# A trunk of two layers on one core: Toeplitz blocks loaded from a shifted copy in DRAM, or straight from the kernel table

## Chip, cores, metric

One core of a Trainium2 chip. The metric is device time in microseconds (us) of one execution, as the median of the runs; lower is better.

## What is computed

Two layers on 512 tokens of width 1024, each `x + Mixer(RMSNorm(x))`, and a final RMSNorm. The first mixer is chunked gated linear attention. The second is a state-space layer (S5) of 128 groups; a group has 16 channels and 64 complex states. The change concerns the second one alone:

```python
lam_bar = jnp.exp(lam * dt)
b_bar = ((lam_bar - 1.0) / lam)[..., None] * b_cplx
bu = einsum('blgi,gpi->blgp', u32, b_bar)              # 16 inputs of a group -> 64 states
_, states = associative_scan(combine, (a, bu), axis=1) # s_t = lam_bar * s_(t-1) + bu_t
y = real(einsum('blgp,gip->blgi', states, c)) + d_skip * u32
y = gelu(y); y = y * sigmoid(y @ w_glu + b_glu); y = y * silu(z)
out = y @ w_out
```

## The kernel before

**The S5 layer in pieces of eight tokens.** The 512 tokens are cut into 64 pieces of T = 8. The groups are worked in NB = 16 blocks of GB = 8 groups. For a group, `bm` (128 x 128) takes the 8 x 16 inputs of a piece to its states, a scan runs over the 64 pieces, `cm` (128 x 128) takes the state before a piece to its outputs, and `gh` (128 x 128) takes the inputs of a piece to the outputs of the same piece. `gh` is a Toeplitz matrix: its entry depends on output channel, input channel and the distance in time. All three are held as two fp16 parts (high and low), so a product is three matmuls (`three16`, lines 769 to 774).

**The kernel table.** `kz` in DRAM has for each group and input channel a row of 480 fp16 numbers: 224 zeros (distances below zero, written by `zero`, line 961) and then 256 values, the 8 distances x 16 outputs x (high, low). `finish_z` (line 1326) computes the 256 for one block: the four small products `pk` on TensorE at line 1333, evictions on ACT and VectorE, the split into `kf` on POOL (lines 1342 to 1345), and one 64 KB store at line 1346. The row of `gh` for input channel i at time j is row i of the table, read from 32 * j numbers further left: 256 numbers, 512 bytes.

**The shifted copy.** `gcopy` (line 1349) reads those 128 shifted rows for each of a block's 8 groups and writes them to `gmd`, an array in DRAM of 512 KB a block: one DMA, DRAM to DRAM. `load_b` (line 596) later loads a block of `gmd` through `loadw` (line 566) into SBUF, as one DMA of 512 KB (line 581), or for the first NPRE = 3 blocks as two of 256 KB (line 578), into the smaller `big` buffers. The same `loadw` loads `bm`, the scan tables `tab`, and `cm`.

**What sets the order.** The tables are prepared while the first layer runs: `plan` (lines 356 to 365) lists steps F (`finish_b`, `compute`, `load`), Z (`finish_z`, and `gcopy` of the block before), E (scan tables) and a last G (`gcopy` of block 15), and `hook` (line 369) takes steps at a rate (`RATES`) as TensorE's first-layer products are emitted. `compute` is POOL's work; its inputs `lpt`, `s_bi`, `s_xc`, `pp` come by DMA (lines 1276 to 1282). The second layer runs in steps too: `LAS`, `LBS` and so on give the step of each block's `load_a` (`bm`, `tab`), `load_b` (`gh`, `cm`), `sA` (first product, scan), `sB` (line 817: the products with `gh` and `cm`, then the store of y to `yd` on ACT's queue), `load_y` (line 834: y comes back from DRAM in another layout) and `sC` (line 839: GELU on ACT). Within a step, `rank` puts `load_y` ahead of `load_a` and `load_b`. Blocks 0 to 2 are loaded during the last of the first layer (lines 673, 674, 685 to 687). From this program order a compile-time scheduler, with an estimate of its own of how long each operation and transfer takes, fixes the order of instructions on each engine; an engine then works strictly in that order. Nearly all DMAs are issued by SP, also in order: one that waits holds all behind it. Weights go through `wunit` (line 178): two raw buffers (`wraw`), split into eight (`whl`) by ACT and VectorE or POOL.

Of the kernel before, what the change touches and what calls it, by code (L numbers as in the profile page):

```python
# [11 lines left out]
F16 = mybir.dt.float16  # L12
# [9 lines left out]
P = 128  # L22
# [9 lines left out]
T = 8  # L32
NC = SEQ // T
GB = 8
NB = 16
KW = 15 * 16
# [18 lines left out]
NPRE = 3  # L55
# [6 lines left out]
SEQ0 = 'h0 u h2 u h4 u s h6 u x0 t x1 q0 q1 t'  # L62
GP = 4
RATES = [0.84, 0.84, 0.88, 0.94, 0.94]
LOWS = {'F': 0, 'Z': 20, 'E': 100, 'G': 0}
ETABS = [2, 3, 3, 3, 3, 3, 3, 3, 4, 4, 4, 4, 4, 4, 4, 7, 8]
POS = [[0, 0, 1, 2, 1, 2, 3, 1, 2, 3, 3], [0, 1, 1, 3, 4, 5, 6, 5, 5, 7, 9], [0, 1, 3, 4, 4, 5, 6, 5, 6, 8, 8], [1,
    1, 4, 4, 4, 5, 6, 6, 6, 6, 8], [0, 0, 0, 0]]
# [22 lines left out]
def trunk_kernel(  # L91
# [6 lines left out]
    V, A, G, S, PE = nc.vector, nc.scalar, nc.gpsimd, nc.sync, nc.tensor  # L98
    sb = ctx.enter_context(tc.tile_pool(name="sb", bufs=1))
    ps = ctx.enter_context(tc.tile_pool(name="ps", bufs=1, space=PSUM))  # L100
    dr = ctx.enter_context(tc.tile_pool(name="dr", bufs=1, space=DRAM))
    cnt = [0]

    def T_(shape, tag, bufs, dt=F32):
        cnt[0] += 1
        return sb.tile(shape, dt, tag=tag, name=f"{tag}_{cnt[0]}", bufs=bufs)
# [20 lines left out]
    def q4(dt=F32, n=1024):  # L127
        return T_([P, n], "q4", Q4, dt)
# [204 lines left out]
    prep = S5Prep(tc, dr, C_, T_, PT, ident, q4, q2, big, tmp, s_bi, s_xc)  # L333
# [4 lines left out]
    @contextmanager  # L338
    def later(n):
        tc.cur_priority += n  # L340
        yield
        tc.cur_priority -= n
# [13 lines left out]
    plan = []  # L356
    ne = 0
    for cb in range(NB + 1):
# [3 lines left out]
        while ne < ETABS[cb]:  # L362
            plan.append(("E", ne))
            ne += 1
    plan.append(("G", NB - 1))
    pace = [0.0]
    phase = [0]

    def hook():
        pace[0] += RATES[phase[0]]  # L370
        while pace[0] >= 1:
            pace[0] -= 1
            if plan:
                st = plan.pop(0)
                with later(LOWS[st[0]]):
                    prep.step(mark, *st)
# [188 lines left out]

    def loadw(cb, src, dt=F16):
        n = 1024 if dt == F16 else 512
        if src is prep.gmd:
            srcs = [src[cb, 4 * k:4 * k + 4].rearrange("g p w -> p g w") for k in range(2)]
            full = src[cb].rearrange("g p w -> p g w")  # L570
        else:
            srcs = [src[cb][:, k * n:(k + 1) * n] for k in range(2)]
            full = src[cb]
        fit = (lambda t: t.rearrange("p (g w) -> p g w", w=2 * P)) if src is prep.gmd else (lambda t: t)
        if cb < NPRE:
            w = [T_([P, n], "big", BIG, dt) for _ in range(2)]
            for k in range(2):
                S.dma_start(out=fit(w[k]), in_=srcs[k])
            return w
        t = q4(dt, 2 * n)  # L580
        S.dma_start(out=fit(t), in_=full)
        return [t[:, :n], t[:, n:]]

    def wsel(w):
        return [[w[k][:, g * P:(g + 1) * P] for g in range(GB)] for k in range(2)]

    def gsel(w):
        v = [t.rearrange("p (g q k) -> p k g q", k=2, g=GB // 2) for t in w]
        return [[v[g // 4][:, k, g % 4] for g in range(GB)] for k in range(2)]

    def load_a(cb):
        t = st_[cb]
        t["bm"] = wsel(loadw(cb, prep.bmd))
        t["cs"] = loadw(cb, prep.tab, F32)

    def load_b(cb):
        t = st_[cb]
        t["gh"] = gsel(loadw(cb, prep.gmd))
        t["cm"] = wsel(loadw(cb, prep.cmd))

    v0 = ([], [])
# [35 lines left out]
    for h in range(NH):  # L637
# [26 lines left out]
        if h == 0:  # L664
            weave([z], tk)
            prep.zero()
            tick()
        elif h < NH - 1:
            weave([proj_v(h, *v), proj_out(h - 1, prev, range(2)), z], tk)
        else:  # L670
            weave([proj_v(h, *v), proj_out(h - 1, prev, range(1)), z], tk)
            weave([proj_out(h - 1, prev, (1,))], [(POS[4][b], trn, b) for b in range(4)])
            load_a(0)
            load_b(0)
# [7 lines left out]
    for n in range(2):  # L682
        phase[0] = 3
        weave([proj_out(NH - 1, prev, (n,))], [])
        for b in range(n + 1, NPRE if n else min(2, NPRE)):
            load_a(b)
            load_b(b)
        build_hT(xts, gc2, h23, l23, range(4 * n, 4 * n + 4), True, PT if n == 0 else PO)
        for tb in range(NT):
            square(xts[tb][n], ssq[:, tb, n:n + 1])  # L690
            S.dma_start(out=x1d[tb * P:(tb + 1) * P, n * 512:(n + 1) * 512], in_=xts[tb][n])
# [171 lines left out]
    def win():  # L863
        for c in ORDER:
            n = int(c[1])
            if c[0] == "u":
                yield from dense_tok(s_wu[n], h2, l2, lambda tb, acc, n=n: ev_u(n, tb, acc), late=False, pool=True)
            elif c[0] == "z":
                yield from dense_ch(s_wz[n], h2, l2, lambda m, acc, n=n: ev_z(4 * n + m, acc), pool=True)
            else:  # L870
                yield from dense_ch(w_glu[n], yh, yl, lambda m, acc, n=n: ev_g(4 * n + m, acc), pool=True)
# [6 lines left out]
    for b in range(NB):  # L878
        at(TS[b], sT, b)
        at(SRS[b], sR, b)  # L880
        at(A0S[b], sA, b)
        at(SBS[b], sB, b)
        at(SCS[b], sC, b)
        at(LYS[b], load_y, b)
        if b >= NPRE:
            at(LAS[b], load_a, b)
            at(LBS[b], load_b, b)
        at(SGS[b], s5, b)
    phase[0] = 4
    rank = {"sC": 0, "s5": 1, "sB": 2, "sA": 3, "sT": 4, "load_a": 5, "load_b": 6, "load_y": 4, "sR": 7}  # L890
    w = win()
# [22 lines left out]
    for tb in range(NT):  # L914
        for k in range(2):
            S.dma_start(out=f(x1p)[k * 64:(k + 1) * 64, 2 * tb:2 * tb + 2].rearrange("p q d -> p (q d)"),
                        in_=x1d.rearrange("(c j) d -> j c d", j=T)[2 * tb + k])
# [21 lines left out]
class S5Prep:  # L939
    def __init__(self, tc, dr, C_, T_, PT, ident, q4, q2, big, tmp, s_bi, s_xc):  # L940
        self.tc = tc
        self.nc = nc = tc.nc
        self.C_, self.T_, self.PT, self.ident = C_, T_, PT, ident
        self.q4, self.q2, self.big, self.tmp = q4, q2, big, tmp
        self.s_bi, self.s_xc = s_bi, s_xc
        self.kz = dr.tile([NG, 16, KW * 2], F16, name="kz")
        self.bmd = dr.tile([NB, P, 2 * GB * P], F16, name="bmd")
        self.cmd = dr.tile([NB, P, 2 * GB * P], F16, name="cmd")
        self.gmd = dr.tile([NB, GB, P, 2 * P], F16, name="gmd")
        self.tab = dr.tile([NB, P, 2 * GB * NC], F32, name="tab")  # L950
        self.pw = dr.tile([2 * NS, NG, 2 * T], F32, name="pw")
        self.lpt = dr.tile([T, NG, 2, NS], F32, name="lpt")
        self.bcd = dr.tile([2, NS, NG], F32, name="bcd")
        self.r8d = dr.tile([NS, NG], F32, name="r8d")
        self.kdd = dr.tile([NG, 16], F32, name="kdd")
        self.etd = dr.tile([NG], F32, name="etd")
        self.t = 0
        self.ld = {}
        self.res = {}
# [386 lines left out]
        S.dma_start(out=self.kz[cb * GB:(cb + 1) * GB, :, 224:480].rearrange("g i w -> (g i) w"),  # L1346
                    in_=kf.rearrange("p w k -> p (w k)"))

    def gcopy(self, cb):
        src = bass.AP(self.kz.tensor, self.kz[cb * GB].offset + 7 * 32, [[2 * KW, P], [-32, T], [1, 2 * P]])  # L1350
        self.nc.sync.dma_start(out=self.gmd[cb].rearrange("g (i j) w -> (g i) j w", j=T), in_=src)

    def step(self, mark, code, cb):
        with ExitStack() as st:
            for k in ("pe", "act", "dve", "sp"):
                st.enter_context(self.tc.issue_after(mark[k]))
            if code == "F":
                if cb:
                    self.finish_b(cb - 1)
                else:  # L1360
                    self.load(0)
                if cb < NB:
                    self.compute(cb)
                if cb + 1 < NB:
                    self.load(cb + 1)
            elif code == "Z":
                self.finish_z(cb - 1)
                if cb >= 2:
                    self.gcopy(cb - 2)
            elif code == "G":  # L1370
                self.gcopy(cb)
            else:
                self.etab(cb)

# [55 lines left out]
```

## Time and profile before

| | |
|---|---|
| median of 3 runs | 1055.71 us (1053.78 to 1055.98) |
| the profiled execution | 1054.56 us |
| its span, first to last instruction | 1052.9 us |
| mean granted TensorE clock | 0.945 |
| busy: TensorE, VectorE, POOL, ACT | 88%, 68%, 49%, 45% of the span |
| moved by DMA | 205.79 MB, mean 195 GB/s |

The engines are PE (TensorE matmul), PEld (its weight loads), DVE (VectorE), ACT (ScalarE), POOL (GpSimd) and SP (SyncE, which here only issues DMAs). A name such as SPq or ACTq means the engine's queue issuing a DMA. Tile names stand as output<-inputs, with buffer numbers left out, so `q<-gmd` is any load from `gmd` into a buffer of the kind `q4`. The first layer takes about the first 505 us; the blocks of the second run from about 545 to 815, and after that TensorE has the large products of `w_glu` and the output projection.

### The profile page before, as it was taken

To read this page: it belongs to the slowest core of one execution; us is meant where nothing else is said; L and a number is where in the kernel's file an instruction comes from. 1 tells how busy PE (TensorE), PEld (TensorE's weight loads), DVE (VectorE), ACT (ScalarE), POOL (GpSimd) and SP (SyncE) were. 2 spreads that over 40 slices of the span, in tenths; PEclk is the share of its full clock that TensorE was granted. 3 is DMA by queue.
4 is the path that set the end of the run, shared out by engine and by line. 5 is a ranking of instruction groups with operands and counts; after the bars stand their busy time and mean duration, and the time that the engine had idled before them with its cause. 6 is when DMAs were issued, how large, how long until landed. Compare 5 with 4: busy or idle time off the path is not lost. (4 is left out here: it accounts for less than half of the span.)

```text
span 1052.9 us, 13715 instructions
## 1 busy us (share of the span) xinstructions
PE 927.6 (88%) x5019; PEld 720.8 (68%) x5019; DVE 713.8 (68%) x916; ACT 472.2 (45%) x707; POOL 511.0 (49%) x477
## 2 busy tenths in 40 slices
PE   6795966699869796969989999999998999999996
PEld 5573754457646684747777777787777888888885
DVE  5794569957898887978645769789897432424322
ACT  5553343445546455433556684744453332313222
POOL 4164808976897979899973434453314000000000
PEclk9897987999889998989999999999999999999998
DMA  8884466999969899999578447687854323353312
GB/s 256 221 183 100 87 167 185 276 247 262 265 209 250 228 292 273 237 321 317 190 226 259 151 121 250 211 300 252 264 185 140 110 82 99 100 160 100 100 61 80
DMA packets 118707, 205.79 MB, mean 195 GB/s; under 512 B 32400, under 2 KB 69824, under 8 KB 118640
## 3 DMA queue, kind: packets, MB, share of 16 engines
q1 hardware_dynamic: 110208, 180.90, 55.2%
q0 software_dynamic: 5472, 19.02, 10.0%
q10 hardware_dynamic: 2960, 4.99, 1.3%
q8 instruction: 39, 0.64, 0.3%
q14 instruction: 28, 0.23, 0.1%
HBM read 167.69 MB, written 45.59 MB: 203 GB/s over the span
## 5 line engine op out<-in xcount | busy, mean ns | idle before, releaser
L162 DVE TENSOR_TENSOR whl<-wraw,whl 128x1024 fp32r<-128x1024 f32 x77 | 106.6, 1384 | 147.5 <-ACT whl L161 147.3
L161 ACT CAST whl<-wraw 128x1024 fp32r<-128x1024 f32 x100 | 104.7, 1048 | 183.7 <-PE pt L199 46.0
L202 PE MATMUL pd<-whl,actA 128*128 128x512 f32 x384 | 154.6, 408 | 12.9 <-ACT whl L161 9.2
L203 PE MATMUL pd<-whl,actA 128*128 128x512 f32 x384 | 154.2, 402 | 0.0
L204 PE MATMUL pd<-whl,actA 128*128 128x512 f32 x384 | 154.0, 404 | 0.0
L270 POOL TENSOR_TENSOR rstd<-rv,neghalf 128x1 f32<-128x1 f32 (+1 forms) x6 | 5.2, 874 | 248.4 <-DVE rv L269 248.4
L198 PE MATMUL pd<-actA,whl 128*128 128x512 f32 x256 | 101.6, 403 | 3.3 <-ACT u L732 3.1
L200 PE MATMUL pd<-actA,whl 128*128 128x512 f32 x256 | 101.4, 397 | 0.0
L202 PEld LDWEIGHTS pd<-whl,actA 128*128 128x128 f32 x384 | 74.4, 194 | 32.7 <-ACT whl L161 9.2
L202 PE MATMUL pd<-whl,q 128*128 128x512 f32 x192 | 80.3, 419 | 11.7 <-DVE xx L541 5.1
L204 PEld LDWEIGHTS pd<-whl,actA 128*128 128x128 f32 x384 | 73.9, 193 | 18.6 <-issue 2.8
L203 PEld LDWEIGHTS pd<-whl,actA 128*128 128x128 f32 x384 | 73.9, 192 | 17.7 <-issue 2.1
L162 POOL TENSOR_TENSOR whl<-wraw,whl 128x1024 fp32r<-128x1024 f32 x23 | 58.3, 2533 | 52.5 <-ACT whl L161 49.2
L203 PE MATMUL pd<-whl,q 128*128 128x512 f32 x192 | 79.6, 415 | 0.0
L1318 DVE TENSOR_TENSOR q<-q,q 128x1024 f16<-128x1024 f32 x32 | 60.4, 1886 | 12.6 <-ACT q L1317 12.3
L198 PEld LDWEIGHTS pd<-actA,whl 128*128 128x128 f32 x256 | 48.5, 190 | 16.6 <-ACT u L732 5.2
L1293 POOL TENSOR_TENSOR q<-q,q 128x1024 f32<-128x1024 f32 x16 | 43.4, 2709 | 31.7 <-DMA q<-s_bi 29.6
L198 PE MATMUL po<-actA,whl 128*128 128x512 f32 x128 | 52.4, 409 | 5.8 <-ACT whl L185 5.8
L185 ACT CAST whl<-wraw 128x1024 fp32r<-128x1024 f32 x36 | 37.7, 1046 | 44.0 <-PE pd L203 26.4
L200 PEld LDWEIGHTS pd<-actA,whl 128*128 128x128 f32 x256 | 48.4, 189 | 11.2
L204 PE MATMUL pd<-whl,q 128*128 128x512 f32 x128 | 53.7, 424 | 1.4 <-DVE q L165 1.4
L202 PEld LDWEIGHTS pd<-whl,q 128*128 128x128 f32 x192 | 38.4, 200 | 23.6 <-DVE xx L541 6.4
(334 smaller groups left out, 2484.4 us busy)
## 6 DMA issues: line engine op xcount, KB each, us to landing
wraw<-w_glu SPq DMA_DIRECT2D x32, 512.0 KB, 3.4
wraw<-w_v SPq DMA_DIRECT2D x16, 512.0 KB, 5.4
wraw<-w_z SPq DMA_DIRECT2D x16, 512.0 KB, 6.5
whl<-w_z POOLq DMA_DIRECT2D x16, 512.0 KB, 7.9
wraw<-w_out SPq DMA_DIRECT2D x16, 512.0 KB, 6.8
q<-lpt SPq DMA_DIRECT2D x16, 512.0 KB, 6.8
q<-s_bi SPq DMA_DIRECT2D x16, 512.0 KB, 9.5
tab<-q SPq DMA_DIRECT2D x32, 256.0 KB, 4.2
```

Of the source, the lines that this page charges most:

```text
L161: i0 = A.copy(out=dst_hi, in_=src)
L162: i1 = E.tensor_tensor(out=dst_lo, in0=src, in1=f(dst_hi), op=SUB)
L185: A.copy(out=hi, in_=raw)
L198: PE.matmul(acc, lhsT=wh, rhs=ah, start=first, stop=False)
L200: mark["pe"] = PE.matmul(acc, lhsT=wl, rhs=ah, start=False, stop=last).ins
L202: PE.matmul(acc, lhsT=ah, rhs=wh, start=first, stop=False)
L203: PE.matmul(acc, lhsT=ah, rhs=wl, start=False, stop=False)
L204: mark["pe"] = PE.matmul(acc, lhsT=al, rhs=wh, start=False, stop=last).ins
L270: G.tensor_tensor(out=dst, in0=v, in1=neghalf.to_broadcast([P, w]), op=ALU.pow)
L1293: tt(out=m, in0=lp, in1=bb, op=MUL)
L1318: nc.vector.tensor_tensor(out=hl[:, 1], in0=src, in1=hl[:, 0], op=SUB)
```

## The change

`gcopy`, the array `gmd` and the step G go. `load_b` gives `loadw` the table itself; for each of the block's eight groups one DMA of 64 KB reads the 128 shifted rows from `kz` into that group's 256 columns of the SBUF tile. The tiles, their buffers, the matmuls and all step tables stay. The program has 128 loads in place of 19, and 16 copies fewer.

```diff
--- before.py
+++ after.py
@@ -62,7 +62,7 @@
 SEQ0 = 'h0 u h2 u h4 u s h6 u x0 t x1 q0 q1 t'
 GP = 4
 RATES = [0.84, 0.84, 0.88, 0.94, 0.94]
-LOWS = {'F': 0, 'Z': 20, 'E': 100, 'G': 0}
+LOWS = {'F': 0, 'Z': 20, 'E': 100}
 ETABS = [2, 3, 3, 3, 3, 3, 3, 3, 4, 4, 4, 4, 4, 4, 4, 7, 8]
 POS = [[0, 0, 1, 2, 1, 2, 3, 1, 2, 3, 3], [0, 1, 1, 3, 4, 5, 6, 5, 5, 7, 9], [0, 1, 3, 4, 4, 5, 6, 5, 6, 8, 8], [1,
     1, 4, 4, 4, 5, 6, 6, 6, 6, 8], [0, 0, 0, 0]]
@@ -362,7 +362,6 @@
         while ne < ETABS[cb]:
             plan.append(("E", ne))
             ne += 1
-    plan.append(("G", NB - 1))
     pace = [0.0]
     phase = [0]
 
@@ -565,21 +564,20 @@
 
     def loadw(cb, src, dt=F16):
         n = 1024 if dt == F16 else 512
-        if src is prep.gmd:
-            srcs = [src[cb, 4 * k:4 * k + 4].rearrange("g p w -> p g w") for k in range(2)]
-            full = src[cb].rearrange("g p w -> p g w")
-        else:
-            srcs = [src[cb][:, k * n:(k + 1) * n] for k in range(2)]
-            full = src[cb]
-        fit = (lambda t: t.rearrange("p (g w) -> p g w", w=2 * P)) if src is prep.gmd else (lambda t: t)
         if cb < NPRE:
             w = [T_([P, n], "big", BIG, dt) for _ in range(2)]
+        else:
+            t = q4(dt, 2 * n)
+            w = [t[:, :n], t[:, n:]]
+        if src is prep.kz:
+            for g in range(GB):
+                S.dma_start(out=w[g // 4][:, g % 4 * 2 * P:(g % 4 + 1) * 2 * P], in_=prep.toep(cb * GB + g))
+        elif cb < NPRE:
             for k in range(2):
-                S.dma_start(out=fit(w[k]), in_=srcs[k])
-            return w
-        t = q4(dt, 2 * n)
-        S.dma_start(out=fit(t), in_=full)
-        return [t[:, :n], t[:, n:]]
+                S.dma_start(out=w[k], in_=src[cb][:, k * n:(k + 1) * n])
+        else:
+            S.dma_start(out=t, in_=src[cb])
+        return w
 
     def wsel(w):
         return [[w[k][:, g * P:(g + 1) * P] for g in range(GB)] for k in range(2)]
@@ -595,7 +593,7 @@
 
     def load_b(cb):
         t = st_[cb]
-        t["gh"] = gsel(loadw(cb, prep.gmd))
+        t["gh"] = gsel(loadw(cb, prep.kz))
         t["cm"] = wsel(loadw(cb, prep.cmd))
 
     v0 = ([], [])
@@ -946,7 +944,6 @@
         self.kz = dr.tile([NG, 16, KW * 2], F16, name="kz")
         self.bmd = dr.tile([NB, P, 2 * GB * P], F16, name="bmd")
         self.cmd = dr.tile([NB, P, 2 * GB * P], F16, name="cmd")
-        self.gmd = dr.tile([NB, GB, P, 2 * P], F16, name="gmd")
         self.tab = dr.tile([NB, P, 2 * GB * NC], F32, name="tab")
         self.pw = dr.tile([2 * NS, NG, 2 * T], F32, name="pw")
         self.lpt = dr.tile([T, NG, 2, NS], F32, name="lpt")
@@ -1346,9 +1343,8 @@
         S.dma_start(out=self.kz[cb * GB:(cb + 1) * GB, :, 224:480].rearrange("g i w -> (g i) w"),
                     in_=kf.rearrange("p w k -> p (w k)"))
 
-    def gcopy(self, cb):
-        src = bass.AP(self.kz.tensor, self.kz[cb * GB].offset + 7 * 32, [[2 * KW, P], [-32, T], [1, 2 * P]])
-        self.nc.sync.dma_start(out=self.gmd[cb].rearrange("g (i j) w -> (g i) j w", j=T), in_=src)
+    def toep(self, g):
+        return bass.AP(self.kz.tensor, self.kz[g].offset + 7 * 32, [[2 * KW, 16], [-32, T], [1, 2 * P]])
 
     def step(self, mark, code, cb):
         with ExitStack() as st:
@@ -1365,10 +1361,6 @@
                     self.load(cb + 1)
             elif code == "Z":
                 self.finish_z(cb - 1)
-                if cb >= 2:
-                    self.gcopy(cb - 2)
-            elif code == "G":
-                self.gcopy(cb)
             else:
                 self.etab(cb)
```

## Rows read from the trace of the kernel before

**Rows 1.** Windows by stage: start:end, length, busy us of each engine, granted clock, DMA share, GB/s.

```profile
200.00:458.00 258.00, 223.50 (x950) 164.58 (x949) 213.99 (x209) 127.50 (x195) 213.03 (x191) 0.92 0.91 253
458.00:560.00 102.00, 87.39 (x399) 67.99 (x398) 65.73 (x80) 50.97 (x86) 88.85 (x71) 0.92 0.82 257
560.00:800.00 240.00, 224.51 (x1952) 180.37 (x1951) 203.71 (x249) 129.27 (x181) 93.05 (x63) 0.99 0.67 219
800.00:1036.00 236.00, 236.00 (x1077) 190.11 (x1077) 83.45 (x91) 68.85 (x89) 6.74 (x4) 1.00 0.32 99
```

**Rows 2.** Waits of TensorE, 200 to 458 us: total us, times, longest.

```profile
PE pt L1333 <- POOL bh L1311: 7.6, 2, 5.4
PE pt L1333 <- DVE q L1323: 5.9, 1, 5.9
```

**Rows 3.** Waits of POOL, 200 to 458 us.

```profile
POOL q L1302 <- DMA pp<-pw: 13.3, 3, 6.2
...
POOL kf L1344 <- DMA kz<-kf: 6.7, 4, 3.1
```

**Rows 4.** DMA issues by line: KB each, median us from issue to landing.

```profile
gmd<-kz SPq DMA_DIRECT2D x16, 512.0 KB, 5.4
...
q<-gmd SPq DMA_DIRECT2D x13, 512.0 KB, 5.3
...
pp<-pw SPq DMA_DIRECT2D x16, 64.0 KB, 5.7
```

**Rows 5.** Tile gmd: issue durations in ns (least, median, most), first and last start.

```profile
L1351 SPq DMA_DIRECT2D gmd<-kz x16: 527/545/749, 218.9 to 555.9; - x16
L581 SPq DMA_DIRECT2D q<-gmd x13: 370/370/427, 569.1 to 776.7; - x13
L578 SPq DMA_DIRECT2D big<-gmd x6: 371/411/676, 460.8 to 492.7; - x6
```

**Rows 6.** Waits of the SP queue, whole span.

```profile
SPq L1351 <- DMA kz<-kf: 42.7, 11, 7.9
```

**Rows 7.** Timeline of SP, 316 to 332 us: start, us, queue, line, transfer.

```profile
321.21 0.33 SPq L1346 DMA_DIRECT2D kz<-kf  x1
328.60 0.54 SPq L1351 DMA_DIRECT2D gmd<-kz  x1
```

**Rows 8.** Timeline of SP, 125 to 155 us.

```profile
144.75 4.63 SPq L966 DMA_DIRECT2D kz<-tmp  x9
```

**Rows 9.** Timeline of TensorE, 775 to 777 us.

```profile
775.84 0.20 PE L772 MATMUL pt<-q,q 128*128 128x64 f16 x1
```

**Rows 10.** Timeline of SP, 744 to 757 us.

```profile
748.28 0.37 SPq L581 DMA_DIRECT2D q<-gmd  x1
...
750.00 0.47 SPq L836 DMA_DIRECT2D xx<-yd  x1
```

**Rows 11.** Timeline of SP, 457 to 487 us.

```profile
476.09 0.55 SPq L1278 DMA_DIRECT2D q<-s_bi  x1
...
477.31 0.54 SPq L1351 DMA_DIRECT2D gmd<-kz  x1
```

**Rows 12.** Timeline of POOL, 478 to 496 us, in brackets the idle time and its releaser.

```profile
485.67 2.40 POOL L1293 TENSOR_TENSOR q<-q,q 128x1024 f32<-128x1024 f32 x1 [0.41 <-DMA q<-s_bi]
```

**Rows 13.** Timeline of TensorE, 512 to 520 us.

```profile
517.09 0.89 PE L298 MATMUL pt<-ident,xx 128*128 128x128 f32 x4 [2.32 <-DVE actA L165]
```

**Rows 14.** Timeline of ACT, 757 to 800 us.

```profile
760.15 0.72 ACT L841 ACTIVATE big<-xx,mx 128x512 f32<-128x512 f32 x1 [2.57 <-DMA xx<-yd]
...
784.64 0.72 ACT L841 ACTIVATE big<-xx,mx 128x512 f32<-128x512 f32 x1 [4.45 <-DMA xx<-yd]
```

**Rows 15.** Timeline of TensorE, 786 to 796 us.

```profile
792.45 0.19 PE L773 MATMUL pt<-q,q 128*128 128x64 f16 x1 [3.56 <-DVE q L823]
```

**Rows 16.** Timeline of SP, 768 to 792 us.

```profile
776.75 0.37 SPq L581 DMA_DIRECT2D q<-gmd  x1
...
777.79 0.48 SPq L836 DMA_DIRECT2D xx<-yd  x1
```

## The prediction

> **What bounds the kernel now.** I read the windows first. [...] Then the waits of TensorE from 200 to 458: its first two rows, 7.6 and 5.9 us, are the small products of the table preparation, which wait for POOL and DVE [rows 2]; no row of that view names a DMA. The DMAs work at one remove: in the same stretch POOL waits 13.3 us for `pp` and 6.7 us for the landing of a `kz` store [rows 3]. Last the SP queue, which issues nearly every transfer in order.
>
> **What goes: sixteen copies inside DRAM.** Each moves 512 KB and takes 5.4 us to land [rows 4]; 11 of them are issued before 458, 5 from 458 to 556. Each issue holds SP for 0.545 us [rows 5], 8.7 us for all. Each also waits for the store of its own block, and while it waits SP issues nothing: 42.7 us in 11 waits [rows 6]. One such wait: store issued at 321.21, copy at 328.60 [rows 7]. For SP alone that is 51 us. I cost it at almost nothing: what covers it is that TensorE's waits of the stretch are all on engines [rows 2], and that weights are prefetched. What I do count is the traffic. 253 GB/s over 258 us is 65 MB, and the 11 copies are 5.8 MB of it, 9%, right behind the stores and loads that POOL waits for. Ends: 9% of POOL's 20.0 us, 1.8 us, if waits shrink only as bytes do; 13.5 us, TensorE's two waits for preparation, if POOL gets so far ahead that they vanish. I take 4, nearer the low end, because only the larger of the two is POOL's own, the other DVE's.
>
> **What comes: eight 64 KB loads for one of 512 KB (blocks 3 to 15), or for two of 256 KB (blocks 0 to 2).** Bytes and the 512-byte pieces stay the same. The new reads start every 64 bytes, as the copies' reads did; copies and loads of `gmd` land in 5.4 and 5.3 us [rows 4], so I cost the shifted reading at nothing. The added cost is issue time: nine small `kz` stores in a row took 4.63 us of SP, 0.51 each [rows 8], so eight cost 4.1 us, against 0.37 for one load or two times 0.41 [rows 5]. Per block that is 3.7 us more for blocks 3 to 15 and 3.3 for 0 to 2. Each load writes its own 256 columns; TensorE meets eight landings for one, at the first product of each group. No row prices seven waits that are already met; between nothing and 0.2 us a block (one such product takes 0.20 [rows 9]) I take nothing, since the loads come long before their use: the load at 748.28 [rows 10] is for block 13, whose product starts at 775.84 [rows 9], 27.6 us later.
>
> **458 to 560.** Blocks 0 and 1 are loaded here, before SP issues the inputs of the last preparation step: 12 more issues, 6.1 us, less one copy, 0.5, ahead of `s_bi` at 476.09 [rows 11]. POOL starts that step at 485.67, 0.41 us after it became free, the moment `s_bi` landed [rows 12]; its results go over DVE to the wait of 2.32 us before TensorE's transposes at 517.09 [rows 13]. There is no slack in that chain, so 5.6 us late at SP is 5.6 late on POOL. Against it stands the copy at 477.31 [rows 11], issued 1.2 us behind `s_bi` and sharing the engines with it: without it the landing is earlier, by nothing to its own 5.4 us. I take 1.6 and so 4 us later; ends 0 and, where small loads also hold each other up, 8.
>
> **560 to 800.** 13 times 3.7 is 48 us of SP's 240. Queued behind the eight are the `cmd` load, a weight load and the reload of `y`. The first two have cover: the use 26 us away and the split weights ahead of TensorE. The reload has none where ACT already stands waiting for it: before 760.15 for 2.57 us and before 784.64 for 4.45 us [rows 14], after which TensorE waits 3.56 us [rows 15]. Both reloads were issued just behind a Toeplitz load: 776.75 then 777.79 [rows 16], 748.28 then 750.00 [rows 10]. If all eight stay ahead, each comes 3.7 us later, 7.4 in all; if the scheduler, which has the reload as the older work, slips it in between, about nothing. I take one of the two, 3.7.
>
> **Sum**: -4 + 4 + 3.7 = **+3.7 us**. The profiled execution took 1054.56 us (span 1052.9 and 1.66 around it), 1.15 below the median of the three runs, 1055.71; the sum stands on the median: 1059.4, rounded to **1059 us**, slower by 0.3%. A measurement of this kernel tells about 0.2%, 2.1 us, from no change.
>
> **Rivals.**
> - Faster: the preparation was held up by traffic and by SP's 42.7 us, and both waits of 13.5 us go [rows 2]. For it: POOL is busy 83% of 200 to 458 and waits for transfers. Against it: other waits on the same engines (DVE behind ACT) stand next. With 13.5 won, the 4 of the second stretch and half a reload, 1.9: -7.6, so 1048. Chance 0.34, with the milder forms of it.
> - No change: the reloads are slipped in between, POOL's late step is paid by the missing copies, and 4 us are won and lost, or less. 1055.7; chance 0.20.
> - Slower by much more: both reloads late (7.4), the late step at its bound (8), nothing won: +15, 1071. It is the far end of my own case.
> - The change does not do only what it says: the order of all engines is built by a scheduler from its own estimate of transfers, so removing 16 and adding 109 issues can reorder work that the diff does not touch. Either sign; it widens each case by some 3 us and has no chance of its own.
> - The eight loads do not overlap. A 64 KB load like `pp` takes 5.7 us to land, no less than 512 KB in 5.3 [rows 4]; eight one after another are 45.6 us against the 27.6 between issue and use [rows 9, 10], so at least 18 us late, 1074 or more. Against it: the nine stores of [rows 8] were issued 0.51 us apart, far less than a landing. Chance 0.02. [...]
>
> **How the numbers follow.** Slower 0.46 (0.44 my own case, 0.02 loads that do not overlap), faster 0.34, same 0.20. My own case runs from 1058 to 1071. The range leaves out about one in ten on either side: 1047, just under the faster rival's 1048, to 1067, short of the far end.
>
> **What the next profile would show.** Right: no copies, 128 loads from `kz`, SP's waits for `kz` stores gone, eight issues in some 4 us; POOL's waits for `pp` and `kz` smaller; the `s_bi` wait near 485 longer by 4 us; ACT's waits for the `y` reload longer by 3.7 us at one place. I am wrong if TensorE's waits from 200 to 458 lose 8 us or more (the faster rival), if the reloads stand between the eight loads and no PE wait after 560 grows, or if TensorE waits for a Toeplitz load itself.

## The result, and the profile after

The changed kernel takes 1063.34 us (median of 20 runs, 1058.10 to 1074.18) against 1055.63 us for the kernel before (20 runs): a ratio of 1.0076, 95% interval 1.0053 to 1.0099, some 8 us slower. The ratio leaves out the execution of 1074.18, which ran in a slower state. The sign was forecast and the size, 1059, was low by 4 us; the way by which it came about was not the forecast one.

| | before | after |
|---|---|---|
| the profiled execution | 1054.56 us | 1059.76 us, 3.6 under its median |
| its span | 1052.9 us | 1058.1 us |
| mean granted TensorE clock | 0.945 | 0.941 |
| busy: TensorE, VectorE, POOL, ACT | 88, 68, 49, 45% | 88, 67, 47, 45% |
| moved by DMA | 205.79 MB | 197.42 MB |

The 8.4 MB that went are the sixteen copies (16 x 0.524 MB). The windows of the kernel after, by the stages of [rows 1]: length, busy us of PE, PEld, DVE, ACT and POOL, granted clock, DMA share, GB/s.

```profile
200.00:458.00 258.00, 216.41 (x894) 158.65 (x893) 206.35 (x204) 124.99 (x189) 210.24 (x188) 0.89 0.83 227
458.00:560.00 102.00, 87.69 (x401) 67.35 (x400) 65.53 (x85) 45.33 (x82) 77.54 (x68) 0.92 0.76 241
560.00:800.00 240.00, 228.11 (x1970) 183.66 (x1970) 195.84 (x243) 133.39 (x186) 87.56 (x64) 0.99 0.67 212
800.00:1036.00 236.00, 234.20 (x1088) 189.88 (x1085) 89.30 (x95) 71.78 (x94) 13.32 (x8) 1.00 0.33 105
```

The loss is in the first row. The DMA share fell from 0.91 to 0.83, and yet TensorE got through 894 instructions instead of 950, busy 216 us instead of 223, at a clock of 0.89 instead of 0.92. From 560 on it is, if anything, quicker than before. TensorE ends its 1400th instruction at 434.8 us instead of 423.3, so by then 11.5 us are lost. A landmark farther on says nearly the same: the eight one-column products that turn the row scales (line 698 before, 696 after) stand between the two layers. Their line in the view of one source line, with the first and the last start, before:

```profile
L698 PE MATMUL pt<-ident,big x8: 245/245/266, 543.1 to 543.9; 1*128 1x1 f32 x8
```

and after:

```profile
L696 PE MATMUL pt<-ident,big x8: 245/245/266, 551.7 to 552.5; 1*128 1x1 f32 x8
```

The first layer ends 8.6 us later; the rest of the span is 506.4 us (1058.1 - 551.7) instead of 509.8. So the two terms that I had put into the time after 458 are not what was lost: from the 1400th instruction on, the changed kernel is the quicker one. The waits of TensorE from 200 to 458 after, to be held against [rows 2]:

```profile
PE pt L1330 <- POOL bh L1308: 8.8, 1, 8.8
PE pt L407 <- DVE q L165: 7.2, 1, 7.2
PE po L202 <- ACT big L164: 5.3, 2, 4.1
PE pd L203 <- DMA whl<-w_v: 4.2, 1, 4.2
```

and those of POOL, against [rows 3]:

```profile
POOL whl L187 <- ACT q L164: 9.1, 1, 9.1
POOL bh L1306 <- PE pt L1330: 8.6, 2, 6.5
POOL tmp L1340 <- DVE tmp L1336: 6.5, 2, 5.1
...
POOL kf L1341 <- DMA kz<-kf: 2.6, 2, 2.2
...
POOL q L1299 <- DMA pp<-pw: 2.2, 2, 2.1
```

POOL's waits for transfers did what I had hoped: `pp` from 13.3 to 2.2, `kz` from 6.7 to 2.6. But POOL now stands behind ACT, TensorE and VectorE instead, and TensorE waits longer for POOL than before. All of TensorE's waits in this stretch add up to 41.6 us, before to 36.2; those of the small products alone fell, from 13.8 to 8.8, so what grew are its waits for weights and for the engines that split and evict.

Where that wait comes from can be read in POOL's timeline. The small product of a preparation step needs the factor `bh` of its block, which has one buffer. After:

```profile
283.46 3.24 POOL L1290 TENSOR_TENSOR q<-q,q 128x1024 f32<-128x1024 f32 x1 [4.02 <-DVE q L1320]
...
294.18 0.45 POOL L1306 TENSOR_TENSOR bh<-big,BA 128x128 f32<-128x128 f32 x1
...
295.99 1.43 POOL L1308 TENSOR_TENSOR bh<-bh,bh 128x128 f32<-128x128 f32 x1
```

and before:

```profile
284.39 1.39 POOL L1309 TENSOR_TENSOR bh<-big,BA 128x128 f32<-128x128 f32 x1
285.85 1.36 POOL L1311 TENSOR_TENSOR bh<-bh,bh 128x128 f32<-128x128 f32 x1
```

The same `bh` is ready at 287.2 before and at 297.4 after, though POOL waits less for transfers: in the compiled order of the kernel after, the first products of a later step now stand ahead of it, and the first of them waits 4.02 us for VectorE. TensorE, after:

```profile
297.48 1.06 PE L1330 MATMUL pt<-q,bh 128*32 128x256 f32 x2 [8.77 <-POOL bh L1308]
...
311.63 0.63 PE L202 MATMUL pd<-whl,q 128*128 128x512 f32 x1
312.06 0.57 PE L203 MATMUL pd<-whl,q 128*128 128x512 f32 x1
312.46 0.40 PE L204 MATMUL pd<-whl,q 128*128 128x512 f32 x1
312.70 0.40 PE L202 MATMUL pd<-whl,q 128*128 128x512 f32 x1
```

More is lost here than the 8.77 us of the wait. Behind it the 512-column products start 0.43 us apart, up to 312.1; from 312.5 they start 0.24 apart. The granted clock of the two stretches was 0.50 and 1.00:

```profile
297.40:312.40 15.00, 9.59 (x26) 5.57 (x27) 10.37 (x15) 3.11 (x7) 15.00 (x18) 0.50 0.54 167
312.40:330.00 17.60, 17.60 (x78) 11.62 (x77) 15.58 (x16) 10.23 (x15) 15.33 (x14) 1.00 0.42 120
```

The kernel before has a wait of this kind too, of 5.45 us before 300.80, and a granted clock of 0.51 in the 5.0 us behind it.

Of the order: the diff leaves the program order of TensorE, VectorE, ACT and POOL as it was. But the compile-time scheduler builds each engine's order from its own estimate of the transfers. The two traces first differ on SP at 218.9 us, where the kernel before issues its first copy, and on the other engines between 228 and 231. The longest sequence that both traces share has 387 of POOL's 477 instructions, 831 of VectorE's 916 and 4758 of TensorE's 5019.

### The profile page after: what moved, and what is told of

The parts are those of the page before. It is cut to its first block, busy times and chain, and to the rows that moved or that the text cites. A ratio compares the mean times of both kernels' runs of the same rounds, so it can differ in the third digit from the quotient of the medians.

```text
span 1058.1 us, 13800 instructions
## 1 busy us (share of the span) xinstructions
PE 929.9 (88%) x5019; PEld 723.5 (68%) x5019; DVE 704.9 (67%) x916; ACT 471.5 (45%) x707; POOL 499.4 (47%) x477
## 2 busy tenths in 40 slices
DMA packets 103812, 197.42 MB, mean 187 GB/s; under 512 B 33888, under 2 KB 54928, under 8 KB 103744
## 5 line engine op out<-in xcount | busy, mean ns | idle before, releaser
L162 DVE TENSOR_TENSOR whl<-wraw,whl 128x1024 fp32r<-128x1024 f32 x77 | 110.2, 1431 | 157.2 <-ACT whl L161 157.0
L161 ACT CAST whl<-wraw 128x1024 fp32r<-128x1024 f32 x100 | 104.8, 1048 | 203.3 <-PE pd L203 43.5
L202 PE MATMUL pd<-whl,actA 128*128 128x512 f32 x384 | 155.7, 410 | 13.8 <-ACT whl L161 9.2
L202 PE MATMUL pd<-whl,q 128*128 128x512 f32 x192 | 81.6, 426 | 18.7 <-DVE big L165 9.1
L1315 DVE TENSOR_TENSOR q<-q,q 128x1024 f16<-128x1024 f32 x32 | 70.8, 2212 | 23.5 <-ACT q L1314 22.4
L203 PE MATMUL pd<-whl,q 128*128 128x512 f32 x192 | 80.4, 420 | 0.0
L204 PE MATMUL pd<-whl,q 128*128 128x512 f32 x128 | 54.6, 433 | 0.1
```

What stands on the lines that cost most here:

```text
L161: i0 = A.copy(out=dst_hi, in_=src)
L162: i1 = E.tensor_tensor(out=dst_lo, in0=src, in1=f(dst_hi), op=SUB)
L202: PE.matmul(acc, lhsT=ah, rhs=wh, start=first, stop=False)
L203: PE.matmul(acc, lhsT=ah, rhs=wl, start=False, stop=False)
L204: mark["pe"] = PE.matmul(acc, lhsT=al, rhs=wh, start=False, stop=last).ins
L1315: nc.vector.tensor_tensor(out=hl[:, 1], in0=src, in1=hl[:, 0], op=SUB)
```

## The experiments

Three explanations were to be told apart: the eight issues crowd SP (mine); taking the copies out does harm by itself, for instance because SP's waits no longer hold other transfers back; the new compile-time order does the harm.

**e1, the loads alone.** The changed kernel with the copies put back, their target read by nobody (the array, the calls and the step G come back too and are not printed).

```diff
+    def gcopy(self, cb):
+        src = bass.AP(self.kz.tensor, self.kz[cb * GB].offset + 7 * 32, [[2 * KW, P], [-32, T], [1, 2 * P]])
+        self.nc.sync.dma_start(out=self.gmd[cb].rearrange("g (i j) w -> (g i) j w", j=T), in_=src)
```

> The copies stay (their target is no longer read); the Toeplitz blocks come from the table by eight transfers each. The compile-time order of TensorE's work is that of the kernel before for its first 1493 instructions, past 500 us. If the eight issues crowd SP's queue (ahead of the last preparation input and of the y reloads), this run carries the loss: about 1063, +8 us. If the loss comes from taking the copies out (the first layer in another order), this run is within 2 us of the kernel before, 1054 to 1058, with first-layer windows (200 to 458: PE 223, clock 0.92) as before.

Measured: 1053.73 us, ratio 0.998 (0.9949 to 1.0011). The eight issues, as the scheduler places them, cost nothing that can be told from no change.

**e2, the copies gone alone.** One transfer a block (two for blocks 0 to 2), from `cmd`, so that the product is made of other values.

```diff
-            for g in range(GB):
-                S.dma_start(out=w[g // 4][:, g % 4 * 2 * P:(g % 4 + 1) * 2 * P], in_=prep.toep(cb * GB + g))
+            def piece(g0, ng):
+                return bass.AP(prep.cmd.tensor, prep.cmd[cb].offset + g0 * P * 2 * P,
+                               [[2 * P, P], [P * 2 * P, ng], [1, 2 * P]])
...
+                S.dma_start(out=fit(t), in_=piece(0, GB))
```

> The copies go; the Toeplitz blocks are fetched by one transfer (two for blocks 0 to 2) in the same 512-byte pieces from another array written by then, so the Toeplitz product is made of other values. TensorE's order is that of the changed kernel for its first 1541 instructions. If the eight issues are the cost, this run is no slower than before, 1052 to 1056 (my -4). If taking the copies out is the cost, it is slow by about as much as the changed kernel, 1060 to 1064, and the first TensorE product of the second layer's input (line 696) starts near 551 us instead of 543.

Measured: 1062.68 us, ratio 1.0059 (1.0025 to 1.0094), with the same 8.77 us wait for `bh`, here at 298.55. Taking the copies out carries the loss, by itself or by the order that comes with it.

**e3 and e4, one priority changed.** The constant `'Z': 20` becomes 10 in the kernel before and 30 in the changed one.

> The kernel before, with one constant of the order changed (the z half of a preparation step is put 10 instead of 20 behind in the scheduler's priorities): same work, same transfers, another compile-time order. If order by itself is worth several us here, it moves by 3 us or more in either direction (1047 to 1063); if it is worth little, it stays within 2 us of 1055.6.

> The changed kernel with the same constant at 30 instead of 20: same work and transfers, another order. If the 8 us are a matter of the order that the scheduler happened on, some of it comes back or more is lost, 3 us or more away from 1063.3; if they belong to the removal of the copies or to the eight issues themselves, it stays at 1061 to 1066.

Measured: e3 1052.11 us, 0.997 (0.9938 to 1.0001); e4 1066.88 us, 1.0107 (1.0065 to 1.0149). e3 is level with the kernel before, near the faster edge; e4 lost nothing certain and won nothing back.

**e5 and e6, the copies made short.** As e1, with copies of 8 KB in e5 (printed here against e1), and in e6 of 1024 pieces of 4 bytes instead of 512.

```diff
-        src = bass.AP(self.kz.tensor, self.kz[cb * GB].offset + 7 * 32, [[2 * KW, P], [-32, T], [1, 2 * P]])
-        self.nc.sync.dma_start(out=self.gmd[cb].rearrange("g (i j) w -> (g i) j w", j=T), in_=src)
+        src = bass.AP(self.kz.tensor, self.kz[cb * GB].offset + 7 * 32, [[2 * KW, 16], [1, 2 * P]])
+        self.nc.sync.dma_start(out=self.gmd[cb, 0, 0:16], in_=src)
```

> As e1 (eight loads, copies kept), but each copy moves 8 KB instead of 512 KB, from the same array and with the same wait for the block's store; the order of TensorE's products of preparation is like that of the changed kernel (third and fourth step's products 31 matmuls apart or less, the third at matmul 842 instead of 809). If the loss comes from SP no longer being held back by the copies' waits, this run has the waits and is fast: 1052 to 1056. If it comes from the compile-time order, it is slow, 1060 to 1066, with TensorE's wait for bh of some 8 us near 297.

> As e5, but each copy has all its 1024 pieces, of 4 bytes instead of 512 (4 KB a block): bytes of the copies gone, waits kept, and an order in which the third preparation step's products stand at matmul 809 as in the kernel before, the fourth's at 843 and 855. Order theory: no 8 us wait near 297, and 1050 to 1056, the bytes saved counting for at most a few us. If the copies' bytes had mattered to POOL as my faster rival has it, 1045 to 1050. If this run is slow (1060 or more), order is not the cause.

Measured: e5 1078.79 us, 1.018 (1.0118 to 1.0242); e6 1062.35 us, 1.0081 (1.0047 to 1.0116). In both SP still issues sixteen copies and waits for stores ahead of them (27.5 us in e5, 38.1 in e6), so what held SP back is there, and both are slow: the loss does not need the waits to be missing. e5 lies beyond the 1060 to 1066 that I expected, with executions from 1066.65 to 1083.95; why it is so much slower than the changed kernel was not tried. And e6 speaks against the order theory in the narrow form that I gave it: the third step's products stand where they stood before, and the time was not won back.

**e7 and e8, the changed kernel with the bh chain loosened.** In e7 `'Z'` is 50; in e8 `bh` has two buffers.

```diff
-        bh = self.C2([P, GB, 16], "bh")
+        bh = self.T_([P, GB, 16], "bh", 2, F32)
```

> The changed kernel with the z half of a preparation step put 50 instead of 20 behind: no copies, no waits, but the third and fourth step's products at matmuls 811 and 845 and the fifth's at 919, spread as in the kernel before. Order theory: the 8 us wait near 297 goes and the time is that of the kernel before within some 3 us, 1051 to 1058. If SP's missing waits or the missing copies are the cause, it stays at 1061 to 1066.

> The changed kernel with two buffers instead of one for the small left factor bh of the table's product: POOL can make the next step's bh before TensorE's products of the step before. If the loss is the chain product, bh, product through one buffer, the wait of 8.8 us near 297 goes and with it 5 us or more: 1053 to 1059. If bh only stands late in POOL's queue for other reasons, the wait stays and so does the time, 1061 to 1066.

Measured: e7 1063.36 us, 1.0072 (1.0041 to 1.0103); e8 1060.24 us, 1.0042 (1.0013 to 1.0072). The wait of 8.77 us shrank to 5.43 in e7, with others of the kind behind it, and went in e8, where TensorE's timeline has another in its place:

```profile
295.44 0.80 PE L492 MATMUL pt<-big,big 128*128 128x128 f32 x2 [5.35 <-DVE big L162]
```

So the narrow theory, one wait for one buffer, falls: e7 won nothing and e8 no more than half. What was still open was whether the whole order costs it, or the absence of the copies.

**e9 to e11, the same work in another's order.** The order of a build can be held: an order-only edge (no semaphore) from each instruction of an engine to the next, along a list read from another build. So the changed work ran in the order of the kernel before (e9) and in that of e3 (e11), and the work before in the order of the changed kernel (e10).

```diff
+def in_order(tc):
+    ...
+    for e, order in table.items():
+        for k, n in zip(order, order[1:]):
+            tc.add_manual_dep(lists[e][n], lists[e][k].name, no_sync, reason="order")
```

> The changed kernel's work (no copies, eight loads a block), with every engine's instructions held by order-only edges in the order of the kernel before; on SP the copies are left out and the eight loads stand together where the one load stood. If the compile-time order is the cause, it is as fast as the kernel before or a little faster, 1049 to 1057, and the windows from 200 to 458 show PE's clock at 0.92 or more. If the missing copies or their missing waits are the cause themselves, it stays at 1061 to 1066.

> The work of the kernel before (sixteen copies, one load a block), with every engine held in the order of the changed kernel; each copy stands right behind the store of its block on SP, each single load where the first of the eight stood. If the order is the cause, it is as slow as the changed kernel or slower, 1060 to 1070, with TensorE's 8.8 us wait for bh near 297. If the copies' presence is what keeps the kernel before fast, it is at 1052 to 1057.

> As e9, but in the order of e3 (the kernel before with one priority changed), which ran 0.3% under the kernel before. If the order carries over to the changed work, 1047 to 1055, and this is the fastest of all; if the missing copies cost by themselves, 1058 to 1064.

Measured: e9 1067.61 us, 1.0116 (1.0075 to 1.0157); e10 1070.22 us, 1.0154 (1.011 to 1.0199); e11 1061.36 us, 1.007 (1.0039 to 1.0101). By the totals e10 bears the order theory out, and e9 and e11 contradict it. The traces show why: they lose at another place. The first layer of e9 is back, its landmark at 545.6:

```profile
L696 PE MATMUL pt<-ident,big x8: 245/245/266, 545.6 to 546.4; 1*128 1x1 f32 x8
```

while the rest of its span is 520.9 us (1066.5 - 545.6) against 509.8. There the eight loads had been held together, and SP's timeline and ACT's show the reload of y behind them:

```profile
788.56 5.67 SPq L574 DMA_DIRECT2D q<-kz  x8
...
794.90 0.43 SPq L834 DMA_DIRECT2D xx<-yd  x1
```

```profile
769.37 0.72 ACT L839 ACTIVATE big<-xx,mx 128x512 f32<-128x512 f32 x1 [3.83 <-DMA xx<-yd]
799.42 0.72 ACT L839 ACTIVATE big<-xx,mx 128x512 f32<-128x512 f32 x1 [9.98 <-DMA xx<-yd]
```

These are the two places of [rows 14], 2.57 and 4.45 us there. From 545 to 830 us (e9 has one more behind it, 4.4 us before 834), ACT's waits for reloads add up to 23.3 us in e9; before, 15.4; in the changed kernel, whose scheduler put reloads between the loads, 9.7. The rows are from ACT's waits in e9, before and after:

```profile
ACT big L839 <- DMA xx<-yd: 23.3, 6, 10.0
```

```profile
ACT big L841 <- DMA xx<-yd: 15.4, 5, 4.5
```

```profile
ACT big L839 <- DMA xx<-yd: 9.7, 5, 3.0
```

**e12, both at once.** e1 has nearly the order of the kernel before in the first layer, and the scheduler's own mixing of loads and reloads in the second. The changed work was held in e1's order, the copies alone left out.

> The changed kernel's work with every engine held in the order of e1 (which kept the copies, ran level with the kernel before, and has the y reloads standing between the eight loads); on SP only the copies are left out. In e9 the first layer came back (TensorE's instruction 1900 ended at 547 us, 553 in the changed kernel) and the second layer lost, with ACT waiting 27.7 us for y reloads queued behind eight loads instead of 15.4. If those two are all there is, this run is level with the kernel before or faster by what the copies' traffic was worth, 1048 to 1056, y-reload waits near e1's 9.5 us. If taking the copies away costs something by itself, it is at 1059 or more.

Measured: 1047.65 us, ratio 0.9946 (0.9923 to 0.9968). It is faster than both kernels, by some 6 us and some 14. The row of its landmark, and SP's timeline with a reload between the loads:

```profile
L696 PE MATMUL pt<-ident,big x8: 245/245/266, 537.0 to 537.8; 1*128 1x1 f32 x8
```

```profile
744.31 4.01 SPq L574 DMA_DIRECT2D q<-kz  x5
...
749.04 0.38 SPq L834 DMA_DIRECT2D xx<-yd  x1
...
750.56 1.80 SPq L574 DMA_DIRECT2D q<-kz  x3
```

**All of them side by side.** The windows view for 270 to 430 us shows what an order is worth: same 160 us, TensorE's busy time and instruction count first, then PEld, DVE, ACT, POOL, the clock, DMA share, GB/s. Before, e9 and e12:

```profile
270.00:430.00 160.00, 135.95 (x591) 100.83 (x590) 136.78 (x138) 77.30 (x121) 141.16 (x125) 0.91 0.89 252
```

```profile
270.00:430.00 160.00, 136.10 (x584) 101.80 (x584) 142.91 (x140) 77.15 (x121) 140.27 (x125) 0.89 0.82 228
```

```profile
270.00:430.00 160.00, 134.39 (x590) 99.53 (x589) 142.22 (x141) 78.95 (x122) 143.04 (x127) 0.91 0.81 227
```

After, e8 and e10:

```profile
270.00:430.00 160.00, 130.09 (x535) 95.25 (x535) 127.51 (x128) 75.75 (x117) 136.43 (x122) 0.87 0.81 223
```

```profile
270.00:430.00 160.00, 127.90 (x542) 95.23 (x543) 130.49 (x133) 75.31 (x119) 133.47 (x116) 0.87 0.79 217
```

```profile
270.00:430.00 160.00, 126.14 (x517) 92.19 (x517) 114.87 (x118) 72.86 (x113) 129.32 (x112) 0.87 0.85 239
```

584 to 591 instructions in the old order, with copies or without; 517 to 542 in the new ones, with copies (e10) or without. The orders themselves fall apart in the same way: of POOL's 477 instructions, 425 to 477 share the sequence of the kernel before in e1, e3, e9, e11 and e12, and 374 to 391 in the changed kernel, e2, e4 to e8 and e10. e6, which has the third step in its old place, is among the latter with 391, so it was no test of the old order. The same for a fixed amount of work: each trace holds 5019 records of TensorE, and the table takes the time between the ends of two of them by their number, with the idle time in it. Neighbours differ a little between orders, but 550 and 2100 instructions are nearly the same work. Each row is one execution: that of e11 (1067.15) was 5.8 us above its median and that of e7 (1058.21) 5.2 below.

```
                       850th to 1400th     2100th to 4200th    ratio of
                       us     idle us      us     idle us      the runs
before                 150.4  24.1         271.9  14.3
e3                     149.5  25.5         273.6  14.5         0.997
e1                     150.7  22.7         271.2  13.5         0.998
e12                    145.4  21.2         269.5  12.1         0.9946
e9  (loads together)   146.7  20.5         282.3  18.1         1.0116
e11 (loads together)   154.5  29.8         283.0  18.9         1.007
after                  164.5  29.9         268.9  13.0         1.0076
e2                     165.8  32.1         273.1  14.2         1.0059
e4                     165.8  29.6         269.4  11.1         1.0107
e5                     165.4  36.0         271.8  12.3         1.018
e7                     163.5  30.0         266.8  10.9         1.0072
e8                     161.5  31.5         269.3  13.1         1.0042
e10 (copies kept)      172.6  35.9         266.5   9.5         1.0154
```

The first pair of columns knows two kinds of kernel, 145 to 155 us in orders that a scheduler made with the whole copies in sight, 161 to 173 in orders made without them or with short ones; whether the copies then run or not (e9, e11, e12 without them, e10 with them) does not change the kind. Part of the 14 us between before and after is idle time (5.8); in the rest nearly the same products took longer, at a granted clock of 0.87 instead of 0.91 in the windows above. The stretches that the table leaves out are not alike either: up to the 850th the kernel before takes 262.9 us, the changed one 260.3 and e12 256.2, and from the 1400th to the 2100th 158.3, 156.3 and 165.4. So some of a gain or loss in the first columns is given back behind them, and at the landmark the changed kernel is 8.6 us behind the kernel before and 14.7 behind e12. The second pair knows two kinds as well: 267 to 274 us, and 282 to 283 where the eight loads are held ahead of the reloads.

## Why the prediction was right in sign, and where it was wrong

**That 1059 came so near is luck.** None of its three terms is what made the changed kernel slower, and what did was put at no chance.

**Copies, -4: not contradicted, and not shown.** e12 and e1 have the same order and the same loads and differ in the copies. The quotient of their ratios, 0.9946 / 0.998 = 0.9966, is -3.6 us, and by their two intervals it may be anything from -7.6 to +0.4. The traces of other pairs in one order do not agree. At TensorE's 1400th instruction e9 is 4.0 us ahead of the kernel before (419.3 and 423.3), but e11 is 4.9 behind e3 (425.2 and 420.3). Nor did the gain come as I had it, by way of POOL: its waits for transfers from 200 to 458 us add up to 21.9 us in e9 and 21.7 before, and TensorE's waits for the small products to 14.1 and 13.8. No run takes SP's 42.7 us of waits for stores [rows 6] out by themselves; what they cost is in the -3.6. The faster rival's time, 1048, is that of e12, but not by its mechanism: in e12 TensorE still waits 6.7 and 6.6 us for the preparation, where [rows 2] have 7.6 and 5.9.

**What comes, the issues.** I took 0.51 us an issue from small stores [rows 8]. The view of the tile `kz` after gives 0.60 (least, median, most in ns):

```profile
L574 SPq DMA_DIRECT2D q<-kz x104: 514/597/1826, 578.8 to 792.0; - x104
L574 SPq DMA_DIRECT2D big<-kz x24: 514/597/729, 473.9 to 506.4; - x24
```

So a block's eight cost 4.8 us of SP, not 4.1. TensorE never waited noticeably for a Toeplitz load (0.3 us in all in that view), and the rival in which the loads do not overlap is out: e12's second stretch in the table, 269.5 us, is no longer than the 271.9 before. And e1, which exchanges one transfer for eight, has a ratio of 0.998.

**458 to 560, +4: there when the order is held, but the changed kernel did not take that way.** I had SP's order stay as it was. With that order held, e9 shows the term: the last preparation step starts at 489.59 instead of 485.67, 3.9 us later, with the wait for `s_bi` at 4.00 instead of 0.41 us [rows 12]. The number is right and its parts are not: `s_bi` was issued 2.8 us later (478.89, against 476.09 in [rows 11]), not 5.6, and took 10.6 us to land instead of 9.4, though the copy behind it was gone. TensorE lost more than 4: it was 4.0 us ahead at its 1400th instruction and is 2.5 behind at the landmark.

```profile
489.59 2.42 POOL L1290 TENSOR_TENSOR q<-q,q 128x1024 f32<-128x1024 f32 x1 [4.00 <-DMA q<-s_bi]
```

In the changed kernel the scheduler put `s_bi` ahead of the loads, and the same step started without a wait. SP's timeline and POOL's, after:

```profile
460.49 0.55 SPq L1275 DMA_DIRECT2D q<-s_bi  x1
...
473.90 5.09 SPq L574 DMA_DIRECT2D big<-kz  x8
```

```profile
472.34 3.32 POOL L1290 TENSOR_TENSOR q<-q,q 128x1024 f32<-128x1024 f32 x1
```

**560 to 800, +3.7: the same.** The prediction left open whether the scheduler slips the reload in between the eight loads, and took one of two places. It slipped it in at several places, as here after, and ACT's waits for reloads fell by 5.7 us (15.4 to 9.7):

```profile
744.91 6.02 SPq L574 DMA_DIRECT2D q<-kz  x7
750.98 0.59 SPq L834 DMA_DIRECT2D xx<-yd  x1
751.61 0.59 SPq L574 DMA_DIRECT2D q<-kz  x1
```

TensorE's waits from 560 to 800 us fell from 15.4 to 11.9 in all. That was my own sign of being wrong, and by it this term is wrong. Held together (e9), the loads cost more than the 7.4 that I gave as the bound: the second stretch of the table is 10.4 us longer than before (282.3 - 271.9). Ahead of the two late reloads the eight issues took 6.5 and 5.7 us instead of 4.1, reloads were late at more than the two places that I had looked at (5.19 us at 698.37, where before had 2.47), and the granted clock from 560 to 800 us was 0.96 instead of 0.99.

**The step that failed** is the rival that I gave no chance: that the scheduler reorders work which the diff does not touch, "Either sign; it widens each case by some 3 us and has no chance of its own." The changed kernel and e12 execute the same instructions and transfers and differ in order alone: 1.0076 / 0.9946 = 1.0131, about 14 us. The changed kernel is slower because the order that the scheduler built without the copies loses some 14 us, in the first layer by the landmarks (551.7 and 537.0), against which stand the 6 by which e12 beats the kernel before.

**What stays open.** Why that order is worse. It seems to be the copies' length in the scheduler's estimate that changes it: short copies (e5) give an order nearer to that of the changed kernel (424 of POOL's 477 instructions in sequence) than to that of the kernel before (387). But no single wait carries the loss, as e7 and e8 show: with the wait for `bh` gone, e8 waits for VectorE's splits instead, 8.8 us at line 492 and 15.1 at line 407 (7.2 there in the changed kernel). e10 is slower than after by 7 us; there SP waits 77.7 us for stores, 42.7 in the kernel before, and how much of the 7 that makes was not tried.

## What to carry to other kernels

Where a scheduler orders the program, a change of transfers has two effects, its own and that of the order that it sets off; here the second was 14 us, and the first -3.6, which the intervals do not tell from nothing. They can be separated by building the changed work in an old order with order-only edges, and that is also how the gain is kept: the edit that made this kernel 0.8% slower makes it 0.5% faster in a held order (e12). When a term of a forecast is "so many issues ahead of this load", first ask who decides what stands ahead of it.

## What the runs showed of the hardware that I had not expected

One issue of the changed kernel waited 3.2 us for a transfer with which it shares neither data nor buffer. Eight Toeplitz loads in a row took 8.68 us of SP, which 8 x 0.60 doesn't explain:

```profile
773.28 8.68 SPq L574 DMA_DIRECT2D q<-kz  x8
```

SP's waits from 560 to 800 us name scan tables, weights and gains as what these loads waited for:

```profile
SPq L574 <- DMA q<-tab: 7.3, 5, 2.2
...
SPq L574 <- DMA wraw<-s_wz: 3.6, 3, 1.7
...
SPq L574 <- DMA q<-fnorm: 3.2, 1, 3.2
```

In this trace each of the 603 issues of SP and ACT names the semaphore that its landing raises. There are eight of them, taken nearly in turn: in 555 of 595 cases an issue has that of the issue eight earlier. Of the 446 cases where the last landing on the same semaphore can be told, none starts before it; the nearest starts 0.02 us after it. One of the eight loads above started at 780.12, where the transfer before it on its semaphore, a load of `fnorm`, had landed at 780.10; that is the 3.2 us. My estimate from these counts is that eight small loads for one large bring that point nearer for whatever is issued behind them; no run shows it by itself. Whether the chip or the program's own build sets the number eight, no run shows.
